# Four split and three raw weight tiles instead of three and four, and other rates for the row sums, in a trunk layer on one core

## The chip, the cores and the metric

The kernel runs on one core of a Trainium2 chip. The metric is device time in microseconds: 2089.51 us as the median of three runs (2086.68, 2089.51 and 2090.01). The profile is one further execution of the same program with the hardware profiler.

The engines are named as in the profile: PE is TensorE's matmul and PEld its weight load, DVE is VectorE, ACT is ScalarE, POOL is GpSimd, SP is SyncE (here it only starts DMAs). "L135" is line 135 of the kernel before.

## The reference

One layer of a diffusion backbone on 384 tokens (128 context tokens, 256 latent tokens) with 2048 features, everything in float32:

```python
m = silu(cond) @ w_mod + b_mod                     # six rows of 2048 per condition (context, latent)
sh1, sc1, g1, sh2, sc2, g2 = split(m, 6)
h = rms_norm(x, n1) * (1 + sc1) + sh1
q, k, v, u = split(h @ w_in)                       # w_in: 2048 x 4096
na = attend(q, k, v) @ w_na_proj                   # 16 heads: context, or neighbourhood + cached context
fn = real(fft2(u in 4 groups of channels)) @ w_fnet_proj
g_na, g_fn = split(sigmoid(h @ w_gate))
x = x + g1 * ((g_na * na + g_fn * fn) @ w_o)
h2 = rms_norm(x, n2) * (1 + sc2) + sh2
a, g = split(h2 @ w_gate_up)
x = x + g2 * ((silu(g) * a) @ w_down)
```

What the change touches are the weights on their way to TensorE, and four of the six rows of `m`: `g1`, `sc2`, `sh2` and `g2`, in the kernel's numbering the types 2, 4, 3 and 5.

## The kernel before

**Weight units.** All weights are read once, in 464 units of two k-tiles by 512 columns (512 KB of float32; a unit of one k-tile has 256 KB). A unit goes three steps. `load_unit` starts its DMA on SP into a tile `wraw` (tag `raw`, four of them). `split_unit` has ACT cast it to a rounded float32r tile `wh` (L134) and DVE subtract that from the original into the rest `wl` (L135); of each of these there are three. Then TensorE multiplies: every product takes three matmuls, high by high (L138), rest by high (L139), high by rest (L140). The activations are split in the same way into `hH` and `hL`.

**The lead.** `next_unit` hands out the oldest split unit. On the way it splits a further one, starts a further load, and ticks the other work. `loads = Ahead(load_unit, units, 4)` keeps the loads in flight, and the queue `ready` keeps the units that are split but not yet used: two, beside the one in use. A load needs a free `raw` tile, which is free once both the cast and the subtract have read it; a split needs a free `wh` and `wl`, which PE frees with the unit's last matmul.

**Order.** Every engine runs its instructions in the order in which the program emits them; nothing reorders them. What is not a matmul of a unit is written as generators wrapped in `Paced`: a tick adds the rate to a counter, and each whole number reached emits one step.

**The rows of the modulation.** `rows` is such a generator, over the types 2, 4, 3 and 5. A row is computed in two halves of 1024 columns. For each of 16 k-tiles a tile `wmr` of `w_mod` is loaded (SP), and DVE adds it, times silu(cond), into `accr`, once for each condition (L309 for the first k-tile, L311 for the others; some 1.28 us each). After the 32 sums of a half, four matmuls with a matrix of ones (L321) add over the partitions, DVE adds the bias row (L326, `row`), and POOL sends the four pieces to DRAM (L331, `s_row`). After the types 4 and 3, whose rows are norm 2's scale and shift, `columns` reads the rows back with the features on the partitions (POOL, L337, `colr`), PE turns them (L344), and DVE writes the result (L350 for the scale, L348 for the shift).

**Rates.** `RATES` has the number of steps of `rows` per tick in five stages: [0] in the input projection (one tick a unit), [1] through the gates, the Fourier part and the attention, [2] in the branch projections, [3] in the output projection, [4] in the feed-forward part. Where a row is needed, `rows_until(ty)` emits what is left of it at once: before norm 2's shift is used, `rows_until(3)` stands in the program behind `inv_sqrt`, the steps that end with `r` (L159). In the output projection's last two units the rate is zero.

**Stages.** The input projection runs over four groups of k-tiles (`GROUPS`: 1, 2, 4 and 9 k-tiles), since the modulation that its tokens need becomes ready group by group: `mod_cols` loads `wm` tiles of `w_mod` (L365) and sums on PE (L387). In each group it runs over eight chunks of 512 columns. The first group's partial sums are copied to SBUF by ACT and DVE (L633, L635), those of later groups are added there by DVE (L637). From 343.5 us on come the two branches between the gates, to 694 us, the branch projections to 836.5 us, the output projection to 966 us. Norm 2 follows: ACT and DVE make 1 / rms (`r`), PE turns the shift's columns (L344), spreads `r` over the partitions (L1137) and turns the last chunk of x2 (L1093), and `normed` makes the first two k-tiles of the new tokens (L1150 on ACT, L1156 on DVE). The rest of the program is SwiGLU.

Of the kernel before, what the change touches and what calls it, by code (L numbers as in the profile page):

```python
# [34 lines left out]
NL, NC = LAT // 2 + 1, CTX // 2 + 1  # frequencies of the latents and of the contexts up to the middle  # L35
HALF = NL + NC

# k-tiles of the input projection whose modulation is ready together
MODS = [(0, 1), (1, 2), (3, 4), (7, 4), (11, 4), (15, 1)]
GROUPS = MODS[:3] + [(7, 9)]  # L40
ORDER = [6, 7, 0, 1, 2, 3, 4, 5]  # its column chunks: u, q, k, v
DUE = [0, -0.5, 0, 0]
PREP = [1.3, 1.8, 2.3, 2.3]
PAIR = "qk,b,pv,s0 m0,e0 i0,,s1 m1,e1 i1,,t0,v,,t1,,"  # a pair of heads: its work, tick by tick
RATES = [1.455, 0.5, 1.1, 0.937, 0.452]
# [3 lines left out]
def fr(ap):  # L49
    """The float32 view of a float32r tile, for engines other than TensorE."""  # L50
    return ap.bitcast(F32)


class Paced:
    """A generator of work that is emitted step by step between the weight units."""
# [22 lines left out]
class Ahead:  # L78
    """Loads that run ahead of their use: take() hands out the oldest, more() starts another."""
# [11 lines left out]
    def take(self):  # L91
        return self.got.popleft()
# [3 lines left out]
def trunk_kernel(ctx: ExitStack, tc: tile.TileContext, io: dict):  # L96
# [45 lines left out]
    def warm_sqrt():  # L142
        """Has ScalarE load its table of square roots ahead of their use."""
        warm = small.tile([P, 1], F32, tag="warm", bufs=1, name=nm("warm"))
        nc.scalar.activation(out=warm, in_=ones[:, 0:1], func=AF.Sqrt)

    def inv_sqrt(out, ssq, n, shape):
        """1 / sqrt(ssq / n + eps), with one Newton step; step by step between the engines."""
# [27 lines left out]
    def load_unit(w2, r0, c0, n=2):  # L176
        raw = wpool.tile([P, 2, CH], F32, tag="raw", bufs=4, name=nm("wraw"))
# [6 lines left out]
    front, behind = [], []  # Paced work: thrice a unit (before and after its split, halfway), once a unit  # L184

    def split_unit():
        if loads.got:
            _, raw = loads.take()
            H = wpool.tile([P, 2, CH], F32R, tag="wh", name=nm("wh"))
            L = wpool.tile([P, 2, CH], F32R, tag="wl", name=nm("wl"))  # L190
# [8 lines left out]
    def next_unit(late=False):  # L199
        """The next weight unit; splits the one after the next, loads further ahead, ticks the rest."""  # L200
# [34 lines left out]
    # Every row of rpb that is used (dr 4..10), 64 times over with a period of 128: read with a step  # L235
    # of 127, it is the Toeplitz matrix bias[c, kc] = rpb[dr, kc - c + 15].
# [8 lines left out]
    # columns of the modulations: [:, kt, cond], cond 0 context, 1 latent  # L245
# [8 lines left out]
    # the rows of the residual gates come by way of this pool, up to the feed-forward part  # L254
# [3 lines left out]
    with ExitStack() as ph:  # L258
# [12 lines left out]
        def acc_tile():  # L271
            """A bank of all those of sums and of others, where those are free."""
            return next(ring)()
# [5 lines left out]
        def mod_rows(ty):  # L279
            """The rows of a modulation, to DRAM: the sums of silu(c) * w_mod over the k-tiles on VectorE,  # L280
            those over the partitions on TensorE, in four column tiles of (cond, half of the columns)."""
# [51 lines left out]
        def columns(ty):  # L333
            """The columns of norm 2's shift or scale, from its rows."""
# [20 lines left out]
        def mod_cols(groups, alloc, depth, cols):  # L355
            """The columns of norm 1, group by group of k-tiles, the sums on TensorE: four column tiles
            of 32, of (shift | scale, parity of the k-tile); then rows to columns, parities added."""
# [16 lines left out]
            for kt0, n in groups:  # L374
# [31 lines left out]
                # shift + its bias; (1 + scale + its bias) * norm gain  # L406
# [898 lines left out]
```

## Time and profile before

| | |
|---|---|
| three runs | 2086.68, 2089.51, 2090.01 us (median 2089.51) |
| profiled execution, its span | 2086.3 us |
| PE busy | 2051.1 us (98%) |
| DVE busy | 1215.3 us (58%) |
| ACT busy | 761.2 us (36%) |
| subtracts L135 | 464 of 1205 ns in the mean |
| casts L134 | 464 of 1036 ns in the mean |
| row sums L311 | 240 of 1276 ns in the mean |

For the profiled execution the trace gives its span; a device time of that execution apart from its span is not given. A group's row in the profile gives line, engine, operation and tiles, the number of instructions, then busy us and mean ns of one, then the idle time of the engine just before them and what ended most of it. A row of a timeline gives the start, the duration, the instruction, and in brackets the idle time of the engine before it and what ended that. A row of the waits gives the total, the number and the longest.

### The profile page before, as it was taken

The page shows a single profiled execution, that of the slowest core. Times are in us where ns is not written, and L with a number is a line of the kernel's source. Part 1 is how long each engine was busy: PE and PEld are TensorE (multiplying, and loading weights), DVE is VectorE, ACT ScalarE, POOL GpSimd, SP SyncE. Part 2 cuts the span into 40 slices and gives each one's busy share as a digit, 9 for nine tenths or more (in the row PEclk, how much of TensorE's full clock was granted, in tenths as well). Part 3 has the DMA queues.
Part 4 walks back from the last instruction along what each step waited for, and adds up shares of the span by engine and source line. Part 5 has one row for each costly group of instructions (what it writes and reads, how often), then busy time and mean ns, then how long its engine had stood idle before and what let it go on. Part 6 is the DMA issues. An engine that isn't in the chain of part 4 may idle for free.

```text
span 2086.3 us, 27423 instructions
## 1 busy us (share of the span) xinstructions
PE 2051.1 (98%) x10963; PEld 1858.1 (89%) x10963; DVE 1215.3 (58%) x1434; ACT 761.2 (36%) x1154; POOL 59.0 (3%) x105
## 2 busy tenths in 40 slices
PE   6999999999999999998999999999999999999999
PEld 4668888999999999887998899899989998999897
DVE  4634899687886787765544444545454433333456
ACT  5323232456666443334433332223222232223222
POOL 3000000000001000001000000000000000000000
PEclk9999999999999999999999999999999999999999
DMA  9886878677775775754544545445544444444453
GB/s 334 284 322 210 297 248 311 208 208 232 208 214 153 259 244 196 248 178 130 163 148 154 161 153 161 135 152 158 158 155 133 130 122 130 123 131 122 128 165 121
DMA packets 219999, 390.45 MB, mean 187 GB/s; under 512 B 28080, under 2 KB 64960, under 8 KB 219872
## 3 DMA queue, kind: packets, MB, share of 16 engines
q1 hardware_dynamic: 212704, 382.13, 57.8%
q10 hardware_dynamic: 4672, 6.31, 0.8%
q8 instruction: 86, 1.41, 0.3%
q0 software_dynamic: 2496, 0.27, 0.1%
q14 instruction: 41, 0.34, 0.0%
HBM read 371.81 MB, written 20.51 MB: 188 GB/s over the span
## 4 chain that ended last, share of the span: by engine, by line
PE 94%; DVE 2%; DMA 2%; ACT 1%; issue 1%; SPq 1%; DVEq 0%; ACTq 0%
PE mm L138 19%; PE mm L139 19%; PE mm L140 19%; PE at L138 11%; PE at L140 11%; PE at L139 11%; DMA wm<-in_w_mod 1%; PE md L387 1%; DVE accr L311 1%; DMA xc<-in_x_sample 1%; PE at L907 0%; DVE wl L135 0%; PE md L321 0%; SPq L365 0%; PE at L1093 0%
## 5 line engine op out<-in xcount | busy, mean ns | idle before, releaser
L135 DVE TENSOR_TENSOR wl<-wraw,wh 128x1024 fp32r<-128x1024 f32 (+1 forms) x464 | 559.0, 1205 | 709.9 <-ACT wh L134 708.8
L134 ACT CAST wh<-wraw 128x1024 fp32r<-128x1024 f32 (+1 forms) x464 | 480.1, 1036 | 1044.0 <-PE at L139 293.0
L138 PE MATMUL mm<-hH,wh 128*128 128x384 f32 x1216 | 409.1, 336 | 2.5 <-DVE acc L637 1.6
L140 PE MATMUL mm<-hH,wl 128*128 128x384 f32 x1216 | 406.7, 334 | 0.0
L139 PE MATMUL mm<-hL,wh 128*128 128x384 f32 x1216 | 406.5, 334 | 0.0
L311 DVE SCALAR_TENSOR_TENSOR accr<-wmr,csz,accr 128x1024 f32<-128x1024 f32 x240 | 304.4, 1276 | 0.0
L138 PE MATMUL at<-hH,wh 128*128 128x384 f32 x704 | 236.3, 336 | 1.4 <-ACT hH L1150 1.4
L139 PE MATMUL at<-hL,wh 128*128 128x384 f32 x704 | 236.3, 336 | 0.0
L140 PE MATMUL at<-hH,wl 128*128 128x384 f32 x704 | 235.8, 335 | 0.0
L138 PEld LDWEIGHTS mm<-hH,wh 128*128 128x128 f32 x1216 | 228.3, 188 | 5.8 <-ACT gst L978 2.1
L139 PEld LDWEIGHTS mm<-hL,wh 128*128 128x128 f32 x1216 | 228.4, 188 | 0.0
L140 PEld LDWEIGHTS mm<-hH,wl 128*128 128x128 f32 x1216 | 228.3, 188 | 0.0
L138 PE MATMUL mm<-wh,hH 128*128 128x512 f32 x431 | 172.7, 401 | 0.0
L139 PE MATMUL mm<-wl,hH 128*128 128x512 f32 x431 | 168.6, 391 | 1.7 <-DVE wl L135 1.7
L140 PE MATMUL mm<-wh,hL 128*128 128x512 f32 x431 | 168.3, 390 | 0.0
L138 PE MATMUL mm<-wh,cH 128*128 128x512 f32 x352 | 139.3, 396 | 0.0
L140 PE MATMUL mm<-wh,cL 128*128 128x512 f32 x352 | 139.2, 396 | 0.0
L139 PE MATMUL mm<-wl,cH 128*128 128x512 f32 x352 | 139.2, 395 | 0.0
L138 PEld LDWEIGHTS at<-hH,wh 128*128 128x128 f32 x704 | 132.7, 188 | 2.8 <-ACT hH L1150 1.8
L139 PEld LDWEIGHTS at<-hL,wh 128*128 128x128 f32 x704 | 132.6, 188 | 1.1 <-DVE hL L1156 0.7
L140 PEld LDWEIGHTS at<-hH,wl 128*128 128x128 f32 x704 | 132.6, 188 | 0.0
L138 PEld LDWEIGHTS mm<-wh,hH 128*128 128x128 f32 x431 | 81.1, 188 | 30.8 <-issue 9.8
(243 smaller groups left out, 2437.9 us busy)
## 6 DMA issues: line engine op xcount, KB each, us to landing
wraw<-in_w_gate_up SPq DMA_DIRECT2D x176, 512.0 KB, 3.7
wmr<-in_w_mod SPq DMA_DIRECT2D x128, 512.0 KB, 4.3
wraw<-in_w_down SPq DMA_DIRECT2D x88, 512.0 KB, 3.7
wm<-in_w_mod SPq DMA_DIRECT2D x64, 512.0 KB, 7.1
wraw<-in_w_gate SPq DMA_DIRECT2D x64, 512.0 KB, 5.1
wraw<-in_w_in SPq DMA_DIRECT2D x56, 512.0 KB, 5.8
wraw<-in_w_o SPq DMA_DIRECT2D x32, 512.0 KB, 5.4
wraw<-in_w_fnet_proj SPq DMA_DIRECT2D x16, 512.0 KB, 5.9
```

The lines of the kernel that those rows point to most:

```text
L134: nc.scalar.copy(H, x)
L135: nc.vector.tensor_sub(L, x, fr(H))
L138: nc.tensor.matmul(out, aH, bH, start=start, stop=False)
L139: nc.tensor.matmul(out, aH, bL, start=False, stop=False)
L140: nc.tensor.matmul(out, aL, bH, start=False, stop=stop)
L311: nc.vector.scalar_tensor_tensor(out=acc[:, cnd], in0=wm, scalar=sc, in1=acc[:, cnd], op0=ALU.mult, op1=ALU.add)
L387: nc.tensor.matmul(pm[q : q + 32, :w], csz[:, k, :], wm[:, ty, kk + par, :], start=k < 2, stop=k >= KT - 2, tile_position=(0, q), skip_gro ...
```

## The change

Three things change.

- The weights have three `raw` tiles instead of four, and `wh` and `wl` have four instead of three. The loads run three ahead instead of four.
- When the second group of the input projection begins, one more unit is split and one more load started; from there on three split units wait in `ready` instead of two.
- Four of the five rates are different. In the input projection 0.9 row sums are emitted a tick instead of 1.455, in the gates and the attention 0.55 instead of 0.5, in the branch projections 1.3 instead of 1.1, in the output projection 1.0 instead of 0.937.

Comments and docstrings are left out in the changed file too. Lines behind 613 stand three further down there: L637 is L640, L1122 is L1125, L1137 is L1140.

```diff
-RATES = [1.455, 0.5, 1.1, 0.937, 0.452]
+RATES = [0.9, 0.55, 1.3, 1.0, 0.452]
...
     def load_unit(w2, r0, c0, n=2):
-        raw = wpool.tile([P, 2, CH], F32, tag="raw", bufs=4, name=nm("wraw"))
+        raw = wpool.tile([P, 2, CH], F32, tag="raw", bufs=3, name=nm("wraw"))
...
     def split_unit():
         if loads.got:
             _, raw = loads.take()
-            H = wpool.tile([P, 2, CH], F32R, tag="wh", name=nm("wh"))
-            L = wpool.tile([P, 2, CH], F32R, tag="wl", name=nm("wl"))
+            H = wpool.tile([P, 2, CH], F32R, tag="wh", bufs=4, name=nm("wh"))
+            L = wpool.tile([P, 2, CH], F32R, tag="wl", bufs=4, name=nm("wl"))
...
-            loads = Ahead(load_unit, units, 4)
+            loads = Ahead(load_unit, units, 3)
...
             for gi, (k0, n) in enumerate(GROUPS):
                 prep.due, prep.rate = DUE[gi], PREP[gi]
+                if gi == 1:
+                    split_unit()
+                    loads.more()
```

Three places show how the instructions move. The first is PE at the end of the output projection. The last row of `at_8487` is its last matmul, L344 the turn of the shift's columns, L1137 (now L1140) the spreading of `r`, and the first L138 behind them belongs to the feed-forward part. Before:

```order
L139 MATMUL at_8487<-wl_8646,hH_1300_7706 128x512
L140 MATMUL at_8487<-wh_8645,hL_1301_7707 128x512
L344 MATMUL md_8749<-ident,colr_8649 128x32
L1137 MATMUL mm_8752<-ident,r_8739 128x128 x3
L1093 MATMUL at_8798<-ident,x_3_7733 128x128 x3
L138 MATMUL at_8776<-hH_1470_8760,wh_8678 128x384
```

and now:

```order
L139 MATMUL at_8487<-wl_8608,hH_1300_7701 128x512
L140 MATMUL at_8487<-wh_8607,hL_1301_7702 128x512
L321 MATMUL md_8740<-accr_7614,ones 32x512 x4
L344 MATMUL md_8753<-ident,colr_8750 128x32
L1140 MATMUL mm_8756<-ident,r_8730 128x128 x3
L1096 MATMUL at_8802<-ident,x_3_7728 128x128 x3
L138 MATMUL at_8780<-hH_1472_8764,wh_8638 128x384
```

The sums over the partitions of the shift's second half (L321) have come in between the stage's last matmul and L344.

The second is DVE at the same place: `row` is the modulation row (L326), `wl` a unit's rest, `d` and `x_3` the residual of the last chunk, L152 to L159 the steps to `r`, `msh` the shift's columns. Before:

```order
L135 TENSOR_TENSOR wl_8611<-wraw_8494,wh_8610 128x1024
L326 TENSOR_TENSOR row_7440<-row_7440,md_8577 128x512
L135 TENSOR_TENSOR wl_8646<-wraw_8522,wh_8645 128x1024
L135 TENSOR_TENSOR wl_8679<-wraw_8553,wh_8678 128x1024
L1122 TENSOR_TENSOR d_8710<-mm_8485,gb_8520 128x512
...
L158 TENSOR_TENSOR rst_8742<-rst_8742,rsv_8740 128x3
L159 SCALAR_TENSOR_TENSOR r_8739<-rst_8742,rss_8741 128x3
L348 COPY msh_112<-md_8749 128x32
```

and now:

```order
L135 TENSOR_TENSOR wl_8639<-wraw_8554,wh_8638 128x1024
L311 SCALAR_TENSOR_TENSOR accr_7614<-wmr_8447,csz,accr_7614 128x1024
L135 TENSOR_TENSOR wl_8670<-wraw_8585,wh_8669 128x1024
L1125 TENSOR_TENSOR d_8701<-mm_8485,gb_8520 128x512
...
L158 TENSOR_TENSOR rst_8733<-rst_8733,rsv_8731 128x3
L159 SCALAR_TENSOR_TENSOR r_8730<-rst_8733,rss_8732 128x3
L326 TENSOR_TENSOR row_7615<-row_7615,md_8740 128x512
L348 COPY msh_112<-md_8753 128x32
```

Row sums (L311) now go on up to the last subtract ahead of the residual, and the addition of the bias row (L326) has moved from a place ahead of the subtract of the stage's last unit (`wl_8646`) to one behind `r`.

The third is SP, whose queue starts the loads, in the first group of the input projection: `wraw` is a weight unit, of one k-tile (128x512) or of two (128x2x512), `wm` a piece of `w_mod` for the columns of norm 1. Before:

```order
L365 DMA wm_365<-in_w_mod 128x2x512 x2
L178 DMA wraw_368<-in_w_in 128x512
L365 DMA wm_398<-in_w_mod 128x2x512 x2
L178 DMA wraw_401<-in_w_in 128x2x512
L365 DMA wm_431<-in_w_mod 128x2x512 x2
L178 DMA wraw_436<-in_w_in 128x2x512
```

and now:

```order
L365 DMA wm_363<-in_w_mod 128x2x512 x2
L178 DMA wraw_366<-in_w_in 128x512
L365 DMA wm_396<-in_w_mod 128x2x512 x2
L178 DMA wraw_399<-in_w_in 128x512
L365 DMA wm_429<-in_w_mod 128x2x512 x2
L178 DMA wraw_434<-in_w_in 128x2x512
```

Each weight unit stands one place further back against the pieces of `w_mod`: the first unit of two k-tiles now stands behind `wm_429`, where before the second stood behind `wm_431`.

## The prediction

> **What bounds the kernel now.** I read the engines' busy time first, then the chain that ended last, then what TensorE (PE) waited for, then the stretches.
>
> ```profile
> PE 2051.1 (98%) x10963; PEld 1858.1 (89%) x10963; DVE 1215.3 (58%) x1434; ACT 761.2 (36%) x1154; POOL 59.0 (3%) x105
> ...
> PE 94%; DVE 2%; DMA 2%; ACT 1%; issue 1%; SPq 1%; DVEq 0%; ACTq 0%
> ```
>
> ```profile
> PE mm L1137 <- DVE r L159: 3.6, 1, 3.6
> ...
> PE mm L139 <- DVE wl L135: 1.7, 3, 0.8
> PE mm L138 <- DVE acc L637: 1.6, 1, 1.6
> ```
>
> PE is busy for 98% of the span, the chain lies on it for 94%, and the change neither adds nor removes a matmul, a cast, a subtract or a sum: it only moves them. So the time can change only by waits of PE that go or come. The second fence is what PE waited for (total, times, longest, us): the waits that a better order could end on are small. I therefore add up waits, place by place.
>
> ```profile
> 0.00:52.00 52.00, 33.55 (x230) 22.70 (x231) 23.55 (x50) 27.34 (x57) 20.44 (x25) 1.00 1.02 334
> ...
> 190.00:343.50 153.50, 150.93 (x670) 123.23 (x668) 134.10 (x148) 47.20 (x52) 4.36 (x9) 1.00 0.85 285
> ...
> 966.00:1000.00 34.00, 28.54 (x150) 26.66 (x151) 25.83 (x53) 19.87 (x45) 0.00 (x0) 0.90 0.31 94
> ```
>
> The columns are the stretch, its length, then busy us of PE, its weight loads, DVE, ACT, POOL, then the granted clock, the DMA share and GB/s. Three stretches have their own limits: the start, where the DMA engines are full (1.02); the last group of the input projection (190 to 343.5 us), where VectorE (DVE) is busy 134.10 of 153.50 us; and norm 2 (966 to 1000 us), where the granted clock falls to 0.90.
>
> **The last group of the input projection: −3.4 us.** RATES[0] falls from 1.455 to 0.9, and the units are split one further ahead.
>
> ```profile
> 325.77 0.50 PE L139 MATMUL mm<-wl,hH 128*128 128x512 f32 x1 [0.59 <-DVE wl L135]
> ...
> 341.50 0.34 PE L140 MATMUL mm<-hH,wl 128*128 128x384 f32 x1
> 343.47 0.44 PE L138 MATMUL mm<-hH,wh 128*128 128x384 f32 x1 [1.63 <-DVE acc L637]
> ```
>
> ```profile
> 341.55 1.27 DVE L311 SCALAR_TENSOR_TENSOR accr<-wmr,csz,accr 128x1024 f32<-128x1024 f32 x1
> ```
>
> ```profile
> PEld mm L138 <- DVE acc L637: 2.0, 1, 2.0
> PEld mm L139 <- DVE wl L135: 1.8, 2, 1.0
> ```
>
> PE waits here three times for DVE: twice for a rest `wl` (one at 325.77), once for a sum of L637 that stands behind one row sum of 1.27 us. The last fence is what the weight loads waited between 318 and 350 us: 2.0 + 1.8 = 3.8 us, the upper bound. What PE itself idled is 1.63 there, and about 0.9 for the two others (the 1.7 of the first list, less 0.8 at 837 us below): 2.5 us, the lower bound. With 0.9 row sums a tick instead of 1.455, DVE sheds 0.555 × 1.27 = 0.7 us of each unit's work here, and three finished units instead of two stand ahead of PE. All three waits go. I take 3.4, since a start of a matmul is late by the weight load's wait too, if not by all of it.
>
> **The start of the output projection: −1.1 us.**
>
> ```profile
> 837.58 0.50 PE L139 MATMUL mm<-wl,hH 128*128 128x512 f32 x1 [0.75 <-DVE wl L135]
> ```
>
> Here `wl` of the stage's first unit is late by 0.75 us on PE, and its weight load by somewhat more. It is a pure matter of lead: a unit further ahead is a unit of PE time earlier. Bounds 0.75 to 1.2; I take 1.1.
>
> **Norm 2: +7.4 us, the largest term.** A change in proportion decides here where the third row's sums end. In the kernel before they end well ahead of the stage's last matmul:
>
> ```profile
> 950.82 0.68 DVE L326 TENSOR_TENSOR row<-row,md 128x512 f32<-128x512 f32 x1
> ```
>
> ```profile
> 951.80 1.91 POOL L331 DMA_DIRECT2D s_row<-row  x4 [144.01 <-DVE row L326]
> 955.51 0.98 POOL L337 DMA_DIRECT2D colr<-s_row  x2 [1.80 <-DMA s_row<-row]
> ```
>
> ```profile
> DMA to landing us min/median/max: 3.3/3.5/3.7
> ```
>
> ```profile
> 965.54 0.24 PE L344 MATMUL md<-ident,colr 32*128 32x32 f32 x1
> 969.37 0.90 PE L1137 MATMUL mm<-ident,r 128*128 128x128 f32 x3 [3.58 <-DVE r L159]
> ```
>
> ```profile
> 969.16 0.16 DVE L159 SCALAR_TENSOR_TENSOR r<-rst,rss 128x3 f32<-128x3 f32 x1
> ```
>
> The row's last sum is added by DVE at 950.82, POOL sends it out as four pieces to DRAM, waits until they have landed, and reads them back as `colr` at 955.51; those land 3.3 to 3.7 us later, so by 959.4. The turn of `colr` (L344) then finds it there at 965.54 without a wait, and PE waits only for `r`. In the changed order the four sums over the partitions (L321) stand behind the last matmul of the output projection, directly ahead of L344, and the addition L326 stands on DVE behind L159, the step that makes `r`. So the addition cannot start before 969.2, the time at which all of this was over before; and L344 needs the whole way through DRAM after it. Queued behind L344 on PE: the spreading of `r` (L1137), the turns of x2 (L1093), the first matmuls of the feed-forward part. DVE's copy L348 and the tokens' split wait for them; no work of PE remains to hide it.
>
> The way's length: 950.82 to 959.36 is 8.54 us. At 654 us, in the attention, the same way of the other row went so:
>
> ```profile
> 653.96 0.69 DVE L326 TENSOR_TENSOR row<-row,md 128x512 f32<-128x512 f32 x1 [0.23 <-issue]
> ...
> 659.34 0.48 POOL L337 DMA_DIRECT2D colr<-s_row  x1 [0.85 <-DMA s_row<-row]
> ```
>
> ```profile
> DMA to landing us min/median/max: 1.8/1.9/2.0
> ```
>
> That is 659.34 + 1.8 − 653.96 = 7.2 us (the landing row is that of `colr` there). At 969.2 plus 7.2 or 8.54, plus 0.24 for L344, against 969.37, the delay is 7.3 or 8.6 us. The four pieces of 951.80 took, in their own row,
>
> ```profile
> DMA to landing us min/median/max: 1.6/2.1/3.0
> ```
>
> so that the shortest I can make the delay is 6.2 (7.3 less 1.1, with the pieces nearer 1.6 than 3.0), and the longest 9.5 (8.6 and 0.9 for a landing later than any of these). I take 7.4, by the short one: the DMA engines are at 0.31 of their time in 966 to 1000 us, and the weight loads of the next units have landed while PE stands still. L321 itself costs nothing new: its matmuls lie in this wait, and those of another row come out from where they were hidden elsewhere (about 0.95 us each way).
>
> PE also comes back cold:
>
> ```profile
> 972.27 0.69 PE L138 MATMUL at<-hH,wh 128*128 128x384 f32 x1 [1.35 <-ACT hH L1150]
> ...
> 975.19 0.50 PE L140 MATMUL at<-hH,wl 128*128 128x384 f32 x1
> ...
> 976.60 0.34 PE L138 MATMUL mm<-hH,wh 128*128 128x384 f32 x1
> ```
>
> Matmuls of one size start 0.32 us apart up to 975.5, and 0.175 after it. Those ten cost 10 × 0.15 = 1.5 us and are paid already. Another slow stretch would cost as much again: bounds 0 to +1.5. I take +0.2, because in the trace the slow stretch ends some 6 us after the first matmul behind the wait, whatever lay before. The Trainium skill ("TensorE: Matmul & The Clock Gate", What's actually happening) says that the gate knows two states, and that after one idle window of about 3.4 us PE is throttled until about 3.4 us of sustained work. By that rule a wait of 11 us instead of 3.6 us costs no more matmuls than now, and the term would be 0; that the wait of 3.58 us was already enough for 0.50 us matmuls agrees.
>
> **The start: +1.9 us.** With three raw tiles the loads lead by one unit less while the DMA engines are full.
>
> ```profile
> L178 SPq DMA_DIRECT2D wraw<-in_w_in x1: 424/424/424, 37.5 to 37.5; - x1
> ...
> DMA to landing us min/median/max: 9.0/9.0/9.0
> ```
>
> ```profile
> L178 SPq DMA_DIRECT2D wraw<-in_w_in x1: 420/420/420, 40.8 to 40.8; - x1
> ...
> DMA to landing us min/median/max: 9.7/9.7/9.7
> ```
>
> ```profile
> 46.59 1.05 ACT L134 CAST wh<-wraw 128x1024 fp32r<-128x1024 f32 x1
> ...
> 50.26 1.07 ACT L633 COPY acc<-mm 128x512 f32<-128x512 f32 x2
> ```
>
> ```profile
> 51.67 0.40 PE L138 MATMUL mm<-wh,hH 128*128 128x512 f32 x1
> ```
>
> The ninth unit, the first of 512 KB, was issued at 37.5 and landed at 46.5, when ScalarE (ACT) wanted it (46.59). In the changed order its load stands one weight load later on SP's queue, where the tenth was: 40.8 + 9.7 = 50.5, less about 1.4 for a piece of 256 KB instead of 512 in front: 49.1. ACT works in order; so its cast waits 2.5 us, and with it the split of the tokens and the copies of L633 that free PSUM banks (50.26). They end at about 53.4 instead of 51.3, and the unit that PE starts at 51.67 needs one of the banks: 53.4 less 51.5 = +1.9. Bounds: 0, if the banks' slack or a faster landing covers it; +3.2, if the whole 2.5 and a little of the next unit count. I take 1.9.
>
> **The attention, the gates and the branches: +0.8 us.** More of the sums have moved in there (RATES[1] 0.5 to 0.55, RATES[2] 1.1 to 1.3). In the eight pairs of heads one place stands close to its limit:
>
> ```profile
> PEld mm L138 <- ACT gst L978: 0.5, 1, 0.5
> ```
>
> One row sum of 1.27 us now stands ahead there: at most 0.5 + 1.3 = about +2, at best −0.5; the middle is +0.8. Everywhere else the three waits for `wl` counted above are all there are, so a row sum more or less per unit has cover. The feed-forward part keeps its rate: 0. That three raw tiles are enough after the start I read from what the casts waited for:
>
> ```profile
> L134 ACT CAST wh<-wraw 128x1024 fp32r<-128x1024 f32 (+1 forms) x464 | 480.1, 1036 | 1044.0 <-PE at L139 293.0
> ```
>
> Of its idle time before casts, 1044 us, ACT spent the most on PE, which has to free a split buffer, and not on a load: 0 for the raw tile less, and if that cover is gone, a late load costs PE what it did at the start.
>
> **Sum:** 1.9 − 3.4 − 1.1 + 7.4 + 0.8 + 0.2 = **+5.8 us**. It is made against the profiled execution, whose span is 2086.3; its frame would give 2092.1. The median of the runs is 2089.5, 3.2 above that span, so I add the sum to the median: **2095.3 us**.
>
> **Rivals.** *R1, the gains in full and the losses low.* The start is covered (0), the row's way takes 6.2, the attention's place 0: 6.2 − 3.4 − 1.1 = +1.7, to +3.5 with one of the losses: 2091 to 2093, within what can be told from no change (0.2%, 4.2 us, is about the smallest difference that a measurement of this kernel tells). For it: both the start and the attention are estimates by one place each. Against: the norm alone outweighs both gains.
>
> *R2, the other side: the waits for `w_mod` go.* PE waits for modulation weights twice in the input projection, and a weight load fewer now stands ahead of them.
>
> ```profile
> PEld md L387 <- DMA wm<-in_w_mod: 2.5, 3, 1.2
> ...
> PEld md L387 <- DMA wm<-in_w_mod: 4.4, 4, 1.2
> ```
>
> These are 110 to 120 and 145 to 160 us. If all of that 6.9 us goes, and the start costs nothing: 5.8 − 1.9 − 6.9 = −3.0, so 2086.5. It decides from about 2 us of earlier landing on. Against: those loads take buffers that PE itself frees, each 1.2 us of waiting is one load's time, and the DMA engines are full there.
>
> *R3, DVE runs late in the branches.* At 1.3 sums a unit, 1.65 us of DVE a unit where 1.4 was: were the splits there late by 0.5 to 1 us in some eight units, another +5: 2100. Against: PE waited for no `wl` there.
>
> **Chances.** My forecast (the norm's wait outweighs the gains) 0.52, with its own range of 2093.7 to 2099: slower. R1 0.28: the same. R2 0.12: half faster, half the same. R3 0.08: slower. That makes faster 0.06, the same 0.28 + 0.06 = 0.34, slower 0.60. For eight in ten the range takes in R1 and half of R2 below, and the forecast's upper end with R3's lower part above: 2087.5 to 2100.5.
>
> **What would show it.** In the profile after: L344's wait for `colr` of some 11 us at 965 to 977, with L326 right behind L159 on DVE; no wait for `wl` or for the sums of L637 between 318 and 345 us, none at 837; ACT waiting at its cast near 47 us, and PE for a bank near 52. Wrong if L326 starts before `r` is ready, if the way through DRAM takes under 5 us, or if the waits for `w_mod` at 116 and 152 us are gone.

## The result and the profile after

The changed kernel takes 2115.2 us (median of 4 runs, 2112.94 to 2117.32); the kernel before took 2089.8 us beside it (4 runs, 2086.68 to 2090.14). The ratio is 1.0133, with a 95% interval of 1.0122 to 1.0145: slower by 25 us where +5.8 us was forecast. The sign was right, the size was not, and the time lies far outside the range.

The page of the profiled execution (span 2115.5 us; it is the longest of the four):

```profile
PE 2058.4 (97%) x10963; PEld 1863.1 (88%) x10963; DVE 1215.5 (57%) x1434; ACT 760.0 (36%) x1154; POOL 60.1 (3%) x105
...
PE 79%; DVE 9%; DMA 5%; ACT 4%; issue 2%; SPq 1%; ACTq 0%; POOL 0%; DVEq 0%; POOLq 0%
```

The work is the same: PE's 10963 matmuls take 7 us longer, nearly all of it in stretches in which they start further apart at a lower granted clock (cold ones, below); the busy times of DVE, ACT and POOL are the same within 1.5 us. The chain that ended last has left PE: 79% instead of 94%, with DVE at 9% and DMA at 5%. What PE waited for (total, times, longest):

```profile
PE md L344 <- DMA colr<-s_row: 14.1, 2, 9.3
...
PE at L138 <- DVE gl L1037: 5.3, 3, 3.8
PE mm L138 <- ACT gst L981: 3.5, 2, 2.2
...
PE mm L138 <- ACT acc L636: 2.3, 1, 2.3
PE mm L138 <- DVE acc L640: 1.9, 1, 1.9
```

Two waits for `colr` instead of none, new ones for `gl` (L1037 is the product of a gate and a branch's sums, which frees a bank of PSUM, where PE's sums lie), longer ones for `gst`, and one for a bank at the start (L636, the old L633). The waits for `wl` and the wait for `r` are gone from the list, as forecast. In the attention the kernel before had two waits:

```profile
PE at L140 <- DVE uL L135: 0.8, 1, 0.8
PE mm L138 <- ACT gst L978: 0.8, 1, 0.8
```

The stretches after, with the same columns as before:

```profile
190.00:346.00 156.00, 154.14 (x686) 126.60 (x685) 113.06 (x132) 48.21 (x54) 2.45 (x5) 1.00 0.76 250
700.00:720.00 20.00, 15.22 (x74) 14.87 (x73) 6.49 (x9) 9.35 (x13) 5.26 (x11) 0.83 0.74 255
985.00:1030.00 45.00, 33.90 (x175) 30.68 (x174) 30.11 (x60) 21.68 (x50) 5.32 (x11) 0.85 0.25 72
```

DVE is at 113 us instead of 134 in the last group of the input projection; and there is a second stretch in which PE stands still and the granted clock falls: 0.83 at 700 to 720 us.

The matmuls of the weights are the same in the same order in both programs, so the start of one in the one trace, less its start in the other, is how far the changed kernel is behind there. From the two profiled executions, which are 29.2 us apart where the medians are 25.4 apart:

| same matmul, before | after | behind by | what lies since the row above |
|---|---|---|---|
| 29.35 | 27.91 | −1.4 | the first loads (they differ by 1 to 2 us from one execution to another) |
| 54.47 | 57.24 | +2.8 | wait for a bank, 2.3, and cold matmuls |
| 283.85 | 286.08 | +2.2 | an L321 (1.0) that now comes later |
| 330.49 | 331.19 | +0.7 | two waits for `wl` gone |
| 343.47 | 345.47 | +2.0 | L321 (0.95) |
| 687.09 | 694.51 | +7.4 | attention: `gst`, `qz`, `uL` (both kernels have three L321 in that stretch) |
| 701.64 | 714.36 | +12.7 | first wait for `colr` |
| 714.99 | 730.57 | +15.6 | cold matmuls |
| 814.50 | 835.66 | +21.2 | `gl`: 0.7, 1.1 and 4.0; an L321 that now comes later (−1.1) |
| 819.80 | 843.67 | +23.9 | cold matmuls (1.6), L321 (1.1) |
| 943.90 | 965.62 | +21.7 | the wait for `wl` at 837 gone (0.9), an L321 that now comes later |
| 969.37 | 997.82 | +28.4 | second wait for `colr`, at norm 2 |
| last one | | +29.2 | cold matmuls, then nothing more |

**Norm 2** went as forecast, with a shorter way. DVE, POOL and PE there:

```profile
990.82 0.16 DVE L159 SCALAR_TENSOR_TENSOR r<-rst,rss 128x3 f32<-128x3 f32 x1
991.29 0.69 DVE L326 TENSOR_TENSOR row<-row,md 128x512 f32<-128x512 f32 x1 [0.31 <-issue]
```

```profile
992.27 1.91 POOL L331 DMA_DIRECT2D s_row<-row  x4 [139.79 <-DVE row L326]
994.84 0.48 POOL L337 DMA_DIRECT2D colr<-s_row  x1 [0.67 <-DMA s_row<-row]
```

```profile
987.20 1.07 PE L321 MATMUL md<-accr,ones 128*32 128x512 f32 x8
997.60 0.28 PE L344 MATMUL md<-ident,colr 32*128 32x32 f32 x1 [9.34 <-DMA colr<-s_row]
997.82 0.90 PE L1140 MATMUL mm<-ident,r 128*128 128x128 f32 x3
```

The addition stands behind `r`, the way through DRAM takes 997.6 − 991.3 = 6.3 us on quiet queues, and L1140 starts 6.8 us later than by its old distance to the stage's last matmul.

**The same thing happens a second time**, where I had not looked: with the columns of norm 2's scale, at the start of the branch projections.

```profile
698.98 0.68 DVE L326 TENSOR_TENSOR row<-row,md 128x512 f32<-128x512 f32 x1
```

```profile
699.95 1.91 POOL L331 DMA_DIRECT2D s_row<-row  x4 [107.14 <-DVE row L326]
707.21 0.48 POOL L337 DMA_DIRECT2D colr<-s_row  x1 [5.36 <-DMA s_row<-row]
709.45 0.48 POOL L337 DMA_DIRECT2D colr<-s_row  x1 [1.75 <-DMA s_row<-row]
```

```profile
709.03 0.34 PE L140 MATMUL at<-fH,wl 128*128 128x384 f32 x1
714.15 0.28 PE L344 MATMUL md<-ident,colr 32*128 32x32 f32 x1 [4.78 <-DMA colr<-s_row]
714.36 0.69 PE L138 MATMUL mm<-fH,wh 128*128 128x384 f32 x1
```

In the kernel before this turn stood in the attention, and the way took 7.2 us there; PE came to L344 11.7 us after L326 and did not wait. The rates have moved it eight weight units on, into the place where the weights of a new stage and the gates are loaded: the four pieces took 6.2 to 7.5 us to land and `colr` 4.6 to 4.8 us, some 15 us from L326 to L344, where PE was ready after 10.4. So it is the longer way, more than the shorter distance, that made the wait. The matmuls behind it start 0.32 us apart for 5 us, another 2.7 us.

**The casts wait for loads.** What ACT's casts waited for, before:

```profile
ACT wh L134 <- DMA wraw<-in_w_na_proj: 6.8, 2, 3.7
...
ACT wh L134 <- DMA wraw<-in_w_in: 1.4, 1, 1.4
ACT wh L134 <- DMA wraw<-in_w_gate: 1.3, 1, 1.3
```

and after:

```profile
ACT wh L134 <- DMA wraw<-in_w_in: 31.0, 13, 5.2
...
ACT wh L134 <- DMA wraw<-in_w_o: 20.3, 6, 5.6
...
ACT wh L134 <- DMA wraw<-in_w_na_proj: 14.1, 3, 5.9
ACT wh L134 <- DMA wraw<-in_w_fnet_proj: 5.4, 5, 1.8
...
ACT wh L134 <- DMA wraw<-in_w_gate: 4.2, 3, 2.3
```

9.5 us in four waits have become 75 us in thirty. ACT and DVE work in order, so whatever stands behind such a cast waits with it. Whether PE pays for it depends on the place, as e_later will show.

### The profile page after: what moved, and what is told of

The parts are those of the page before. It is cut to its first block, busy times and chain, and to the rows that moved or that the text cites. A ratio compares the mean times of both kernels' runs of the same rounds, so it can differ in the third digit from the quotient of the medians.

```text
span 2115.5 us, 27390 instructions
## 1 busy us (share of the span) xinstructions
PE 2058.4 (97%) x10963; PEld 1863.1 (88%) x10963; DVE 1215.5 (57%) x1434; ACT 760.0 (36%) x1154; POOL 60.1 (3%) x105
## 4 chain that ended last, share of the span: by engine, by line
PE 79%; DVE 9%; DMA 5%; ACT 4%; issue 2%; SPq 1%; ACTq 0%; POOL 0%; DVEq 0%; POOLq 0%
PE mm L138 16%; PE mm L139 16%; PE mm L140 16%; PE at L138 10%; PE at L140 10%; PE at L139 10%; DVE accr L311 3%; DVE wl L135 2%; DMA wm<-in_w_mod 1%; DMA wraw<-in_w_gate 1%; PE md L387 1%; ACT wh L134 1%; DMA wraw<-in_w_in 1%; DMA wraw<-in_w_fnet_proj 1%; DMA xc<-in_x_sample 0%
## 5 line engine op out<-in xcount | busy, mean ns | idle before, releaser
L138 PE MATMUL mm<-hH,wh 128*128 128x384 f32 x1216 | 409.6, 337 | 5.4 <-ACT gst L981 3.5
L311 DVE SCALAR_TENSOR_TENSOR accr<-wmr,csz,accr 128x1024 f32<-128x1024 f32 x240 | 305.1, 1278 | 0.0
L138 PE MATMUL at<-hH,wh 128*128 128x384 f32 x704 | 236.4, 336 | 1.4 <-ACT hH L1153 1.4
L138 PEld LDWEIGHTS mm<-hH,wh 128*128 128x128 f32 x1216 | 228.7, 188 | 9.7 <-ACT gst L981 4.1
L138 PE MATMUL mm<-wh,hH 128*128 128x512 f32 x431 | 172.8, 401 | 2.3 <-ACT acc L636 2.3
L138 PE MATMUL mm<-wh,cH 128*128 128x512 f32 x352 | 139.3, 396 | 0.0
L138 PEld LDWEIGHTS at<-hH,wh 128*128 128x128 f32 x704 | 132.7, 188 | 2.0 <-ACT hH L1153 1.8
L138 PEld LDWEIGHTS mm<-wh,hH 128*128 128x128 f32 x431 | 81.1, 188 | 34.3 <-issue 10.4
```

The source lines that it names most:

```text
L138: nc.tensor.matmul(out, aH, bH, start=start, stop=False)
L311: nc.vector.scalar_tensor_tensor(out=acc[:, cnd], in0=wm, scalar=sc, in1=acc[:, cnd], op0=ALU.mult, op1=ALU.add)
```

## The experiments

Each was timed beside the kernel before, which took 2086.6 to 2086.9 us there (2089.8 beside the changed kernel); the ratios compare.

| run | buffers | rates | ratio | 95% interval |
|---|---|---|---|---|
| changed kernel | new | new | 1.0133 | 1.0122 to 1.0145 |
| e_buffers | new | old | 1.0059 | 1.0044 to 1.0074 |
| e_rates | old | new | 1.0085 | 1.0070 to 1.0100 |
| e_loads3 | old, three loads ahead | old | 1.0051 | 1.0036 to 1.0066 |
| e_start | old, three loads ahead in the first group | old | 1.0015 | 1.0006 to 1.0024 |
| e_later | old, three loads ahead from the second group on | old | 1.0046 | 1.0032 to 1.0059 |
| e_norm2 | new | new, shift in time | 1.0110 | 1.0093 to 1.0127 |
| e_ty4 | new | new, shift and scale in time | 1.0076 | 1.0062 to 1.0089 |
| e_gl | new | as e_ty4, branches 1.1 | 1.0066 | 1.0052 to 1.0080 |
| e_oldbuf | old | as e_ty4 | 1.0041 | 1.0027 to 1.0054 |
| best_a | old | input projection 1.2 | 1.0015 | 1.0006 to 1.0024 |
| best_b | old | input projection 0.9 | 1.0056 | 1.0043 to 1.0068 |
| best_d | old | old but for two rates inside the input projection | 1.0025 | 1.0017 to 1.0034 |

### The two halves apart: e_buffers, e_rates

The changed kernel with the old rates, and the kernel before with the new ones:

```diff
# e_buffers, against the changed kernel
-RATES = [0.9, 0.55, 1.3, 1.0, 0.452]
+RATES = [1.455, 0.5, 1.1, 0.937, 0.452]
# e_rates, against the kernel before
-RATES = [1.455, 0.5, 1.1, 0.937, 0.452]
+RATES = [0.9, 0.55, 1.3, 1.0, 0.452]
```

> The changed buffers (three raw tiles, four split ones, one more unit split at the second group) with the rates of the kernel before. Theory A, the rates did the damage: the row of norm 2's scale is turned after 130 weight units again and that of its shift is summed after 195, so PE waits neither for colr at the branch projections nor beyond r at norm 2; what stays is the start (PE stands 2.3 us for a bank and runs some matmuls cold, +2 to +4 us) less what the earlier splits save (1 to 3 us): 2088 to 2093 us. Theory B, the missing raw tile did it, because casts wait for loads (31 times, 78 us in all, in the changed kernel; 4 times, 9.5 us, before) and ACT and DVE pass the delay on in their order: 2100 us or more, with PE waiting for gl in the branch projections again.

> The buffers of the kernel before with the changed rates. Theory A (the rates): PE waits about 10 us for colr at norm 2 (+6.7 and some cold matmuls), about 5 us for colr at the start of the branch projections (+5 and 2 to 3 us of cold matmuls), and for gl near the end of the branch projections (+4 to +6): 2104 to 2113 us. Theory B (the raw tile): the wait at norm 2 alone remains, +7, less 1 to 3 us in the last group of the input projection: 2093 to 2097 us. Both expect no wait for a bank near 52 us.

Measured: +12 us for the buffers alone, +18 us for the rates alone, together about what both cost. Neither theory is right alone: the rates cost what theory A said, but the buffers cost 12 us where it said 1 to 6; theory B's 2100 us or more was nearly reached (2098.7), but without the wait for `gl` that it named. What PE waited for with the new rates and the old buffers:

```profile
PE md L344 <- DMA colr<-s_row: 14.1, 2, 9.3
...
PE at L138 <- DVE gl L1034: 1.5, 2, 1.0
```

Both waits for `colr` are here in full, so they belong to the rates; the wait for `gl` is 1.5 us instead of 5.3, so its larger part needs the late loads as well: e_buffers, with the old rates, has no wait for `gl` at all. In the last group of the input projection this run gained what was forecast: by the start of the same matmuls 0.9, 0.6 and 1.6 us at 325.77, 330.49 and 343.47, 3.1 us in all, and the wait for the sums of L637 was gone. With the new buffers and the old rates:

```profile
PE mm L138 <- DVE acc L640: 5.6, 1, 5.6
PE md L321 <- DVE accr L311: 4.1, 2, 3.0
```

PE waits for DVE in the very group where the earlier splits were to help: at L321, which needs the row sums to be done, and at the sums of L640.

### One load fewer on its way: e_loads3, e_start, e_later

```diff
# e_loads3: three throughout
-            loads = Ahead(load_unit, units, 4)
+            loads = Ahead(load_unit, units, 3)
# e_start: as e_loads3, and a fourth from the second group on
+                if gi == 1:
+                    loads.more()
# e_later: four as before, and from the second group on three (one load left out of next_unit)
+                if gi == 1:
+                    skip[0] = 1
```

> The kernel before with one number changed: loads run three ahead instead of four (four raw tiles stay, three split ones, the old rates). It shows the shorter lead of the loads alone. If the start is a matter of that lead, ACT's cast near 47 us waits about 2.4 us for its load and PE near 52 us about 2 us for a bank: +2 to +4 us, 2091 to 2094 us by theory A. By theory B the late loads also hold up PE in the input projection and the branches, with only two finished units ahead: 2097 us or more.

> The kernel before with loads three ahead in the first group of the input projection alone; from the second group on four, as ever. The price of the shorter lead at the start by itself: ACT's cast near 47 us waits about 2.4 us for its load, PE near 52 us for a bank, some matmuls run cold: a ratio of 1.001 to 1.002 (+2 to +4 us). If the start is what makes the run with three loads throughout slow, it is near 1.005 as that one.

> The complement: loads four ahead in the first group, three ahead from the second group on. If the late casts in the last group of the input projection (PE waiting for a row sum at its L321 near 284 us and for the sums of L637 at 343 us) carry the rest, the ratio is 1.003 to 1.004, and PE does not wait for a bank near 52 us. If the start carries all, 1.000.

One load fewer, with the old rates, the old three split tiles and four raw tiles allocated, costs 11 us, as theory B said, and as much as all of the changed buffers within the intervals. So the shorter lead of the loads is the price, and the fourth split tile bought nothing that the times can tell. By the traces it did end the three waits for `wl` (1.7 us in e_loads3, none in e_buffers), but e_buffers waits longer in other places: 4.1 instead of 1.8 us at L321, 5.6 instead of 4.3 for the sums. Why these are longer, no run tells. What PE waited for in e_loads3:

```profile
PE mm L138 <- DVE acc L637: 4.3, 1, 4.3
...
PE mm L138 <- ACT acc L633: 2.4, 1, 2.4
PE md L321 <- DVE accr L311: 1.8, 1, 1.8
```

The start is 3 us of it (e_start), the later part 10 us (e_later); the two add up within their intervals. By the start of the same matmuls nearly all of the later part is lost in the last group of the input projection: e_later stands 0.5 us ahead of the kernel before at 283 us and 7.6 behind at 360, by an L321 near 284 us that waits for its row sums, by the sums of L637 at 343, and by 2.3 us of cold matmuls behind the second wait. Its casts wait for their loads 39 us in that group, and 62 us behind it; but there PE loses only 0.7 us more. Late casts cost PE time where DVE, behind them, has hardly any room (134 of 153.5 us busy). In e_start ACT's cast shows the mechanism as it was predicted, and so does that of the changed kernel, below it:

```profile
48.06 1.04 ACT L134 CAST wh<-wraw 128x1024 fp32r<-128x1024 f32 x1 [2.48 <-DMA wraw<-in_w_in]
```

```profile
48.73 1.04 ACT L134 CAST wh<-wraw 128x1024 fp32r<-128x1024 f32 x1 [2.44 <-DMA wraw<-in_w_in]
```

### The two turns in time: e_norm2, e_ty4

```diff
# e_norm2, against the changed kernel
-RATES = [0.9, 0.55, 1.3, 1.0, 0.452]
+RATES = [0.9, 0.55, 1.3, 1.15, 0.452]
# e_ty4: 1.03, and the scale's columns in a generator of their own, one step a unit, five units later
+                    if ty == 4:
+                        behind.append(Paced(late_columns()))
+                        yield
+                        continue
```

> The changed kernel with one rate changed again: 1.15 instead of 1.0 in the output projection, so that the shift's second half is summed after 195 units as before and its addition stands ahead of the last unit's subtract. If the wait at norm 2 is what the order made of it, PE waits for r alone (some 3.6 us) and the time falls by 6 to 8 us against the changed kernel: 2107 to 2109 us. A rival, that the DMA way of the row is late there for another reason (busy queues), leaves it at 2113 or more.

> The changed kernel with both turns of columns brought in time: the scale's columns are turned six weight units later (144 instead of 138 units used), by work of their own beside the rows, and the output projection's rate is 1.03, so that the shift's last sum stands seven units ahead of its turn. If PE's wait for colr at the start of the branch projections and the cold matmuls behind it are worth the 5.3 + 2.4 us of the trace, this takes them off beside the 7 of norm 2: a ratio of about 1.0075 to the kernel before (2102 to 2104 us where that one takes 2087). If the wait only moves (the landing is late because the queues are full, or another wait comes after it), the ratio stays at 1.010 or more.

With the shift's sums done in time, PE waits there for `r` again, and not for `colr`:

```profile
987.93 0.24 PE L344 MATMUL md<-ident,colr 32*128 32x32 f32 x1
991.76 0.54 PE L1140 MATMUL mm<-ident,r 128*128 128x128 f32 x3 [3.58 <-DVE r L159]
```

By the start of the same matmuls, L1140 gains 6.8 us on the changed kernel just there; the times say 1.0110 against 1.0133, some 5 us where 6 to 8 were expected, with the intervals overlapping a little. With the scale's turn in time as well, the ratio is 1.0076, as expected, and the two turns together are worth 1.0133 − 1.0076 = 0.0057, or 12 us. The trace also shows something given back: 5.2 us of waiting and 2.7 us of cold matmuls of the changed kernel are gone at its 709 to 720 us, and a few units behind, PE waits for `gl`, with another 2.9 us of cold matmuls behind that:

```profile
720.66 0.69 PE L138 MATMUL mm<-aH,wh 128*128 128x384 f32 x1 [4.46 <-DVE gl L1048]
```

The repair itself makes this wait. With the scale's columns in work of their own, the next row's sums begin at once, and their first loads (`wmr`) are started just where the new stage's loads are. DVE stands still for them, with the subtracts and the product for `gl` behind it:

```profile
709.18 0.75 DVE L309 TENSOR_SCALAR accr<-wmr,csz 128x1024 f32<-128x1024 f32 x1 [9.47 <-DMA wmr<-in_w_mod]
```

The longest such wait in the changed kernel is 1.4 us; in e_gl and e_oldbuf, which have the same repair, it is 6.4 and 9.5 us. So the 12 us are rather a lower bound. The waits for `gl` further on are down to at most 1.1 us each. One caution on such readings: up to 343 us the changed kernel, e_norm2, e_ty4 and e_gl run the same instructions, and yet their traces lie up to 4.4 us apart there, with PE's wait for a bank near 52 us between 1.0 and 2.4 us and its wait for the sums of L640 near 343 between 0.6 and 1.9.

### The branch projections: e_gl, e_oldbuf

```diff
# e_gl, against e_ty4
-RATES = [0.9, 0.55, 1.3, 1.03, 0.452]
+RATES = [0.9, 0.55, 1.1, 1.2, 0.452]
# e_oldbuf: e_ty4's rates and its late columns in the kernel before
```

> As the run with both turns in time, and with 1.1 row sums a unit in the branch projections as before the change, 1.2 in the output projection. If PE's wait for gl near the end of the branch projections (4.0 us and some 1.2 us of cold matmuls) comes from 1.3 sums a unit on DVE, it goes and the ratio falls by 0.002 to 0.003 against that run, to about 1.005. If it comes from casts that wait for their loads (three raw tiles), it stays, at 1.007 to 1.008.

> The buffers of the kernel before with the changed rates and both turns of columns in time (1.03 in the output projection, the scale's columns turned nine units after the row). If the two turns and the buffers carry what the change costs, little is left: 1.001 to 1.003, from sums that have moved into the attention less the saving in the input projection. If the wait for gl in the branch projections comes from the rate and not from late loads, it is there too, and the ratio is 1.004 or more.

Fewer row sums in the branches change the ratio by −0.0010, within the intervals: not settled by the time. By the traces the waits for `gl` fall from 6.7 to 4.9 us in e_gl, but all of that lies in the wait behind the late `wmr` (4.5 and 2.4 us); the later ones are 2.2 and 2.5 us. In e_oldbuf PE waits 2.8 us for one `wl` and 1.4 us for `gl`, both behind its late `wmr`, and 0.3 us for `gl` later. So these two runs say little of the rate of the branches. What tells are the first runs taken together: 1.5 us of waits for `gl` with the new rates alone, none with the new buffers alone, 5.3 us with both. It takes both, though which of the rates, no run separates. In the changed kernel one sees how. The chain that ends last goes through two late loads of `w_fnet_proj` (from 793.7 and 805.3 us) into DVE, and there DVE's order puts three row sums, with a subtract between them, ahead of the product that frees the bank:

```profile
830.33 1.28 DVE L311 SCALAR_TENSOR_TENSOR accr<-wmr,csz,accr 128x1024 f32<-128x1024 f32 x1
...
832.66 2.48 DVE L311 SCALAR_TENSOR_TENSOR accr<-wmr,csz,accr 128x1024 f32<-128x1024 f32 x2
835.05 0.55 DVE L1037 TENSOR_TENSOR gl<-gl,at 128x384 f32<-128x384 f32 x1
```

e_ty4 less e_oldbuf, 0.0035 or 7 us, is one price of the buffers with the new rates; the changed kernel less e_rates gives another, 0.0048 or 10 us. With the old rates it was 12 us, and the intervals do not tell the three apart. But the place has moved: between 283 and 360 us of the kernel before e_buffers loses 12.5 us against it, while the changed kernel, whose DVE has fewer sums there, gains 1.3. What e_oldbuf still has over the kernel before, 8.6 us, comes by its trace from the attention and the branches: it is 4.5 us ahead at 343 us of the kernel before (1.2 of it from the first loads) and 1 us behind at 687. The saving of the input projection is spent there and more, in waits for `gst`, 3.6 us instead of 0.8, `uL` and others. Of the 6 us that it loses in the branches, 4.5 lie at the two waits behind the late `wmr`, and so belong to the repair.

### Is there a better proportion? best_a, best_b, best_d

```diff
# best_a and best_b: old buffers, late columns as in e_ty4
-RATES = [1.455, 0.5, 1.1, 0.937, 0.452]
+RATES = [1.2, 0.5, 1.1, 1.1, 0.452]     # best_a
+RATES = [0.9, 0.5, 1.3, 1.3, 0.452]     # best_b
# best_d: the kernel before, with 1.65, and 0.95 in the last two column chunks of the last group
+                    if gi == len(GROUPS) - 1 and ci == ORDER[6]:
+                        rows.rate = 0.95
```

> The buffers of the kernel before, its rates but for 1.2 instead of 1.455 in the input projection, the scale's columns turned nine units after their row's sums, and 1.1 in the output projection to make up for it. If what the lower rate saves in the last group of the input projection (3 to 4.7 us in the run with the rates alone) can be had without the waits that it brought further down, the ratio is 0.998 to 0.9995 (2083 to 2086 us where the kernel before takes 2087). If a sum that moves into the attention stands in the way there wherever it stands, 1.000 to 1.003.

> As the run before in this list, with 0.9 in the input projection and 1.3 in the branch and the output projections; 0.5 in the attention as in the kernel before. All of the saving in the input projection (4.7 us) less one to two us of waits for gl in the branches: 0.998 to 1.000. If 1.3 sums a unit cost there what they do with three raw tiles (5 us): 1.000 to 1.002.

> The kernel before with its row sums dealt out otherwise inside the input projection alone: 1.65 a unit up to the last two column chunks of the last group, 0.95 in these, so that all that comes later stands where it stood. If the three waits for DVE at 325, 330 and 341 us come from the sums beside the last chunks' work, they go (2.5 to 3.8 us) and nothing is given back: a ratio of 0.998 to 0.9988 (2083 to 2084.5 us where the kernel before takes 2087). If the higher rate makes DVE late earlier, 0.999 to 1.001.

None is faster than the kernel before; best_a came out as its second case said, best_b and best_d slower than either of theirs. best_a is 4.0 us ahead at 378 us, but 1.3 of that come from the first loads and 1.1 from an L321 that only stands later; it has lost all of it by 687, in the attention. best_b is 7 us ahead at 378 us (2.0 and 1.1 of it by the same two); it loses 4 us in the attention and 8 us, with 1.3 sums a unit, at an L321 that waits 5.3 us for its row sums at the end of the branches. best_d moved the sums within the input projection alone and was to end three waits; it ended the two for `wl`, but the third grew:

```profile
PE mm L138 <- DVE acc L639: 4.1, 1, 4.1
```

and the cast ahead of it shows why:

```profile
340.44 1.04 ACT L134 CAST wh<-wraw 128x1024 fp32r<-128x1024 f32 x1 [6.00 <-DMA wraw<-in_w_gate]
```

What ends last there is a load of the first gate weights, 8.6 us under way, started right behind the writing of the last projections; the row sum that I had taken for the cause stands behind it, between the subtract and the sums, with 1.2 us. In the changed kernel a load of these weights ends last as well. The chain of its last-ended waits between 325 and 350 us, in order of time (start, us, what):

```profile
333.87 8.54 DMA wraw<-in_w_gate
...
342.51 1.06 ACT wh L134
...
343.59 1.23 DVE wl L135
344.82 0.61 DVE acc L640
...
345.47 0.44 PE mm L138
```

The load, the cast, the subtract and the sums stand one behind the other, and from the load on no row sum is among them here. Ahead of it there are: the load starts right after the subtract at 332.6 us, which frees a raw tile, and that subtract stands behind row sums on DVE.

## Why the prediction was wrong

By its own terms:

- **Norm 2, +7.4 us: right.** 6.8 us by the start of L1140, and 0.7 us of matmuls behind it. That the cold matmuls after a longer wait cost hardly more than after the short one (+0.2 said) held.
- **The start, +1.9 us: right in its mechanism, under-sized.** The cast waited 2.44 us (2.5 said), PE 2.3 us for the bank; 1.6 us of cold matmuls behind it were not in the sum. By the time of e_start it is 3 us. That the 2.5 came out so well is in part luck: the 1.4 us taken off for 256 KB has no row behind it (at the 334 GB/s of that stretch they are 0.8 us), and by the rows shown the copies would end at 51.3 + 2.5 = 53.8 against a matmul at 51.67, so +2.1 and not +1.9.
- **The start of the output projection, −1.1 us: right** (−0.9). The earlier splits did it: the wait is gone in e_buffers too, and 0.6 us of it stay in e_rates.
- **The last group of the input projection, −3.4 us: half.** The two waits for `wl` went (1.5 us); the third stayed, 1.9 instead of 1.6 us in this trace, since in the changed kernel a late load decides it. With four raw tiles the new rates did end it.
- **The attention, the gates and the branches, +0.8 us: the step that failed.** 5.4 us in the attention, 5.2 of waiting and 2.7 of cold matmuls at the scale's turn, 5.8 and 1.6 at `gl`: about 21 us where 0.8 was put. I priced one place there by one row, at 654 us, and called it the only one; the list of PE's waits before already had `gst` and `uL` there, 0.8 us each, which no sentence of the sum took up. I did not ask the question that had carried the norm's term, how far ahead of its turn a row's last sum stands and what the queues are like there, a second time for the other row that goes the same way. The rates move both.
- **Three raw tiles, 0 outside the start: wrong.** That step rested on a group's row, which names only the releaser that most of the idle time is owed to. It says nothing of the few casts at which a load is late, and PE pays for those in the last group of the input projection, where DVE is nearly full. One load fewer is 10 us after the start by itself (e_later).
- A wait was priced by its length alone, but for norm 2. At the start, at the scale's turn and at `gl` it was followed by 1.6 to 2.7 us of slow matmuls.

Of the rivals, R3 (DVE late in the branches) had the right place for a part of it, with chance 0.08 and 5 us; R1 and R2 fell: none of the losses stayed low, and PE's waits for `w_mod` are 3.0 us instead of 2.6 (the 6.9 us of R2 were waits of weight loads; PE itself stood 1.4 us there). The sign came out as forecast, and by the term that was to carry it, but over two thirds of the loss lie in terms that the sum had at next to nothing.

## What to carry to other kernels

When a change moves work by rates, find every consumer that waits for the moved work, and for each one count how far ahead of it the last producer now stands and what else is on the queues there; one that is found is a reason to look for its sisters. A repair moves work too: the one tried here put the next row's first loads into the very place that it had freed. A tile moved from one stage of a pipeline to the next is not free because the stage behind it waits on average: look at the waits that are already owed to the first stage, however few, since these grow, and at whether the engine behind has room to make them good. And a saving in a stage where an engine is nearly full is worth only what the stages that take the work over leave of it; here the attention took back all of it.

## What the runs showed of the hardware

How long a wait makes PE cold is not one number. In the changed kernel, after 4.78 us of waiting at 714 us, matmuls of one size started 0.32 us apart for 5 us, and after 3.8 us at 835 us for some 3.2 us. Of shorter waits, that of 2.4 us for a bank in e_start was followed by 3 us at a granted clock of 0.52:

```profile
53.00:56.00 3.00, 3.00 (x14) 1.36 (x12) 1.92 (x3) 2.49 (x4) 0.00 (x0) 0.52 0.86 296
```

but after 2.8 us for one `wl` in e_oldbuf the clock stayed at 1.00, and so it did after 2.2 us at 517 us in the changed kernel. The Trainium skill ("TensorE: Matmul & The Clock Gate", What's actually happening) says that the array is throttled after an idle window of about 3.4 us and freed after about as much sustained work, and that the window runs freely, whatever the kernel does. The two long waits agree with that; that a wait of 2.4 us, shorter than a window, was enough once does not. In the changed kernel these stretches come to nearly all of the 7 us by which PE's busy time is longer.

The same transfer took very different times by its place in the program: the pieces of a row landed 1.6 to 3.0 us after their start on POOL ahead of norm 2 in the kernel before, and 6.2 to 7.5 us after it at the start of the branch projections in the changed one, where a new stage's weights and gates are loaded:

```profile
DMA to landing us min/median/max: 6.2/6.2/7.5
```

The columns read back landed after 1.7 us at norm 2 (990 to 1000 us; the DMA engines are at 0.25 of their time in 985 to 1030 us) and after 4.6 to 4.8 us at 707 to 714 us (0.74). The Trainium skill ("DMA: Bandwidth & Descriptors", Latency and other measured facts) gives about 2 us of fixed cost and says that it grows with the load on the memory; the direction agrees with that, and at norm 2 the size too, while the 4.6 to 7.5 us at 700 us are two to four times the 2. A way through DRAM has two such legs, and at 700 us it came to 15 us from L326 to L344.

Beside the cold stretches, matmuls of 128x384 start 173.3 ns apart through most of the traces, and 176.7 ns apart in some stretches, with a granted clock of 1.00 by the profile (in best_a from 718 to 817 us, some 1.9 us of its time; in the kernel before from 795 to 828). No run tells what brings it on.

What stays open: whether a fourth split tile beside four raw ones would be worth anything; no run has both.
